# Expert capacities in multiples of 8 and 16, and row gathers rounded up to 16 rows, in a mixture-of-experts block

## The chip, the cores and the metric

The kernel runs on one core of one Trainium2 chip. The metric is the device time of one execution in microseconds (us). A run's profile is one execution of the program, recorded by the hardware profiler; its span is the time from the first to the last instruction of that record.

## The reference

One layer on 2048 tokens of width 1024, in float32. A mixer (a short gated convolution and a gated DeltaNet) and its output projection are added to `x`; then comes a hierarchical mixture of experts with a residual, and a last RMSNorm. What the change touches is the mixture:

```
group  = argmax(h @ router_group_w)                  # 4 groups
top 2  = top_k(softmax(h @ router_expert_w in group), 2)   # 8 experts in a group, 32 in all
gate   = group_prob * top_p / sum(top_p)
out[t] = sum over its 2 experts of gate * ((silu(h[t] @ w_gate[e]) * (h[t] @ w_up[e])) @ w_down[e])
y      = rms_norm(x + out)
```

The 2048 tokens give 4096 pairs of token and expert. Each of the 32 experts has 6.29 MB of float32 weights (1024x512 twice, 512x1024 once), 201 MB in all, and each is read once.

## The kernel before

The mixer takes roughly the first 1150 us. The change acts on what follows.

**Places.** Experts are ranked by their number of tokens, and the list `CAPS` (line 725) says for each rank how many places ("columns") the program computes, whatever the data: the first three ranks have 128, rank 3 has 216, and it falls to 112 for rank 31. (The first three are experts picked early from half of the tokens; a list of overflow blocks at the end of the program takes what doesn't fit. In this execution that loop runs no block.) A rank with more than 128 places has two chunks, one of 128 rows and one of the rest. There are 51 chunks: 13 ranks have one, 19 have two. Places without a token carry a row number past the last token: gathers clip it to token 2047, scatters skip it.

**Order.** The ranks run as jobs in this order, big and small ones in turn, so that ranks 29, 30 and 31 come last:

```
0 1 2 28 3 27 4 26 5 25 6 24 7 23 8 22 9 21 10 20 11 19 12 18 13 17 14 16 15 29 30 31
```

**One job**, in the order of its data:

- `load_part` (line 757): SP loads the expert's weights in 20 steps through ten staging buffers `mst` of 512 KB; ACT and DVE split each into two f16 halves (`split`, line 91; profile lines 92 and 93), `wgu` and `wd`. A load is issued when its buffer is free. Jobs ahead of the current one are loaded while it computes.
- `gather` (line 1046): POOL issues one indirect DMA for each chunk that fetches the token rows (4 KB each, both f16 halves) from `h2_d` into `xr` (line 1050), one row to a partition, and one for each chunk that fetches the gates `gs` (line 1055).
- `turn` (line 1059): TensorE transposes the rows into `xT` (line 1066), DVE copies them out.
- `gate_up` (line 1071): 192 matmuls with weights as the stationary operand and `n` columns of `xT` moving (line 1081), `n` being the rank's places. ACT and DVE make `ac` from the result.
- `down` (line 1107): a rank with one chunk takes `ac` as the stationary operand and moves 512 columns of `wd` (24 matmuls, line 1116); `n` is then no number of moving columns. A rank with two chunks has 96 matmuls with `n` moving columns (line 1151) and transposes back (line 1138). ACT scales the result by the gate into `yo` (lines 1125, 1142).
- `add` (line 1091): POOL issues one indirect DMA for each chunk that adds `yo` to the rows of `acc_d` in memory (line 1094).

ACT, DVE and POOL work each in their own program order.

**The end.** When rank 30 has been scattered, its tokens, those of rank 29 and of rank 31 are gathered from `acc_d` again, one gather for each rank with as many rows as it has places (`rows_of`, line 1420; rank 31's tile is `mst`, those of 29 and 30 are called `end`). Behind these on POOL's queue stand eight gathers of 128 rows for other tokens (`load_late`, line 1391, tile `xw`), and SP stores half of the first eight tiles at that time. ACT squares the tiles in the order `end` of 29, `end` of 30, four of `xw`, rank 31's, four of `xw`; DVE normalises; the stores follow. The last three stores are indirect DMAs on POOL, for ranks 29, 30 and 31 (`store_rows`, line 1431), and each waits until the one before it has landed.

Of the kernel before, what the change touches and what calls it, by code (L numbers as in the profile page):

```python
# [38 lines left out]
def hybrid_block(ctx, tc, x, mix_g, w_in, ca_w, ca_g, dn_w, a_log, dt_bias, dn_g, w_out,  # L39
# [675 lines left out]
    if dbg.get("stop") == "y":  # L715
# [6 lines left out]
    NST = 2  # L722
    C1 = P

    CAPS = [C1, C1, C1, 216, 188, 176, 172, 164, 160, 156, 152, 148, 148, 144, 144, 144, 140, 136, 136, 136,
            132, 132, 128, 128, 124, 124, 124, 120, 120, 120, 116, 112]
    NB2 = 2 * NE
    LAST = 3
    ACS = 4.0
# [63 lines left out]
    V.memset(on16, 1.0)  # L793
    iot = rt.tile([P, max(CAPS)], F32, name="iot")
    G.iota(iot, pattern=[[1, max(CAPS)]], base=0, channel_multiplier=0, allow_small_or_imprecise_dtypes=True)
    mhalf = rt.tile([P, 4], F32, name="mhalf")
# [3 lines left out]
    caps = rt.tile([NE, NE], F32, name="caps")  # L800
    for r, c in enumerate(CAPS):
        if r == 0 or CAPS[r - 1] != c:
            G.memset(caps[:, r:], float(c))
# [8 lines left out]

    CM = max(CAPS)
    tabT = psB.tile([NE, CM], F32, name="tabT", tag="b")
    tabE = rt.tile([NE, CM], F16, name="tabE")
    tabG = rt.tile([P, NE, 2], I32, name="tabG")
    tabS = rt.tile([P, NE, 2], I32, name="tabS")
    gix = rt.tile([P, NE, 2], I32, name="gix")
# [221 lines left out]
    class Job:  # L1040
        def __init__(self, key, chunks):
            self.key, self.chunks = key, chunks
            self.n = sum(c[3] for c in chunks)
            self.base = None

    def gather(J, pool, tag, end=S):
        J.xr, J.gs = [], []
        for ix, gx, sx, cw in J.chunks:
            xr = pool.tile([P, 2, KT, P], F16, name="xr", tag=tag)
            G.indirect_dma_start(out=xr[0:cw].rearrange("p a k c -> p (a k c)"), out_offset=None, in_=h2_d[0:end, :],  # L1050
                                      in_offset=IO(ap=ix, axis=0))
            J.xr.append(xr)
        for ix, gx, sx, cw in J.chunks:
            g = o2.tile([P, 1], F32, name="gs", bufs=6)
            G.indirect_dma_start(out=g[0:cw], out_offset=None, in_=gt_d[0:end * NE, :], in_offset=IO(ap=gx, axis=0))  # L1055
            J.gs.append(g)
        yield 1
# [280 lines left out]
    for r in order:  # L1338
        ch = []
        for i, cw in enumerate((min(CAPS[r], P), CAPS[r] - P)):  # L1340
            if cw > 0:
                ch.append((tabG[0:cw, r, i:i + 1], gix[0:cw, r, i:i + 1], tabS[0:cw, r, i:i + 1], cw))
        jobs.append(Job(r, ch))

    def fetch(J):
        yield from gather(J, o1, "hh")
# [239 lines left out]
```

## Time and profile before

| what | value |
|---|---|
| three timed runs | 1956.95, 1954.14, 1949.02 us (median 1954.14) |
| the profiled execution | 1948.9 us, its span 1947.1 us |
| mean granted TensorE clock | 0.962 of full speed |
| memory traffic | 330.27 MB, mean 170 GB/s |
| busy share of the span: TensorE matmuls, DVE, ACT, POOL | 90%, 72%, 52%, 22% |

The jobs take the time from some 1165 us to the end of the span. "Granted clock" is the share of TensorE's full speed that the throttle allowed. "DMA share" is the mean busy share of the core's 16 DMA engines; the time of overlapping packets can take it above 1. "Landing" is the time from an indirect DMA's issue to its data being there; the profile has it for about half of them.

### The profile page before, as it was taken

The page shows a single profiled execution, that of the slowest core. Times are in us where ns is not written, and L with a number is a line of the kernel's source. Part 1 is how long each engine was busy: PE and PEld are TensorE (multiplying, and loading weights), DVE is VectorE, ACT ScalarE, POOL GpSimd, SP SyncE. Part 2 cuts the span into 40 slices and gives each one's busy share as a digit, 9 for nine tenths or more (in the row PEclk, how much of TensorE's full clock was granted, in tenths as well). Part 3 has the DMA queues.
Part 4 walks back from the last instruction along what each step waited for, and adds up shares of the span by engine and source line. Part 5 has one row for each costly group of instructions (what it writes and reads, how often), then busy time and mean ns, then how long its engine had stood idle before and what let it go on. Part 6 is the DMA issues. An engine that isn't in the chain of part 4 may idle for free.

```text
span 1947.1 us, 41829 instructions
## 1 busy us (share of the span) xinstructions
PE 1752.6 (90%) x16221; PEld 1199.0 (62%) x16221; DVE 1403.5 (72%) x2713; ACT 1007.2 (52%) x1676; POOL 426.7 (22%) x375
## 2 busy tenths in 40 slices
PE   6789999999999999999999969999899999999840
PEld 5455555555555554444454438888788899999730
DVE  8889888888888745322344768777778888888732
ACT  5655434444444424211233637766667767777621
POOL 1321111121111100000000013223322344344343
PEclk9889999999999999999999979999999999999975
DMA  4122001001001105002255967999999999999873
GB/s 143 67 69 53 11 15 46 16 13 46 20 11 37 36 19 165 28 12 60 98 175 189 346 233 258 334 308 306 303 320 359 354 335 340 351 341 317 285 225 142
DMA packets 203597, 330.27 MB, mean 170 GB/s; under 512 B 44590, under 2 KB 98935, under 8 KB 203394
## 3 DMA queue, kind: packets, MB, share of 16 engines
q1 hardware_dynamic: 178738, 271.20, 40.9%
q0 software_dynamic: 20128, 47.30, 9.5%
q10 hardware_dynamic: 4528, 9.06, 1.2%
q8 instruction: 129, 2.11, 0.4%
q14 instruction: 74, 0.61, 0.1%
HBM read 276.05 MB, written 54.82 MB: 170 GB/s over the span
## 4 chain that ended last, share of the span: by engine, by line
PE 29%; DMA 20%; DVE 8%; issue 5%; ACT 5%; POOL 1%; SPq 1%; ACTq 0%; DVEq 0%; POOLq 0%
PE acc L134 11%; DMA mst<-in_w_up_dram 10%; PE a L1081 8%; DMA mst<-in_w_down_dram 5%; PE a L988 5%; DMA mst<-in_w_gate_dram 3%; DVE wgu L93 3%; ACT wgu L92 2%; DVE wd L93 1%; PE pn L548 1%; DMA end<-acc_d,tabG 1%; ACT yo L1142 1%; DMA mst<-acc_d,bix 1%; PE pl L1138 1%; SPq L766 1%
## 5 line engine op out<-in xcount | busy, mean ns | idle before, releaser
L134 PE MATMUL acc<-hT,whl 128*128 128x512 f16 x2640 | 635.3, 381 | 0.2 <-DVE hT L203 0.2
L134 PEld LDWEIGHTS <-whl 128*128 128x128 f16 x2640 | 252.9, 99 | 248.4 <-issue 11.4
L1081 PE MATMUL a<-xT,wgu 128*128 128x128 f16 (+17 forms) x6144 | 394.7, 227 | 3.3 <-DVE sl L1088 2.4
L1081 PEld LDWEIGHTS <-wgu 128*128 128x128 f16 x6144 | 389.3, 99 | 9.5 <-issue 3.5
L93 DVE SCALAR_TENSOR_TENSOR wgu<-mst,gw,wgu 128x1024 f16<-128x1024 f32 x256 | 317.5, 1276 | 19.9 <-ACT wgu L92 17.6
L92 ACT ACTIVATE wgu<-mst,gw 128x1024 f16<-128x1024 f32 x256 | 280.8, 1139 | 36.0 <-DMA mst<-in_w_up_dram 33.7
L988 PE MATMUL a<-wo,yb 128*128 128x512 f16 x768 | 176.3, 381 | 0.0
L93 DVE SCALAR_TENSOR_TENSOR wd<-mst,wd 128x1024 f16<-128x1024 f32 x128 | 154.2, 1215 | 3.6 <-ACT wd L92 3.5
L1094 POOL DMA_INDIRECT acc_d<-yo,tabS x50 | 95.9, 1918 | 265.9 <-ACT yo L1142 191.8
L92 ACT ACTIVATE wd<-mst 128x1024 f16<-128x1024 f32 x128 | 131.3, 1047 | 24.3 <-DMA mst<-in_w_down_dram 24.1
L1151 PE MATMUL a<-ac,wd 128*128 128x144 f16 (+12 forms) x1824 | 136.9, 230 | 4.9 <-ACT ac L92 3.9
L1151 PEld LDWEIGHTS <-wd 128*128 128x128 f16 x1824 | 124.4, 98 | 8.3 <-issue 6.5
L988 PEld LDWEIGHTS <-yb 128*128 128x128 f16 x768 | 72.2, 98 | 79.6 <-issue 3.0
L294 DVE SCALAR_TENSOR_TENSOR cv<-raw,pcol,cv 128x512 f32<-128x512 f32 x144 | 117.1, 815 | 1.6
L1050 POOL DMA_INDIRECT xr<-h_d,tabG x51 | 61.5, 1206 | 179.2 <-PE t L1066 159.0
L1088 DVE SCALAR_TENSOR_TENSOR sl<-a,sl 128x128 f32<-128x128 f32 (+17 forms) x128 | 38.3, 300 | 78.1 <-ACT sl L1087 77.6
L1087 ACT ACTIVATE sl<-a 128x128 f32<-128x128 f32 (+17 forms) x128 | 35.7, 280 | 108.9 <-PE a L1081 108.9
L1116 PE MATMUL pl<-wd,ac 128*128 128x512 f16 (+4 forms) x312 | 78.6, 397 | 6.1 <-ACT ac L92 4.8
L382 DVE TENSOR_TENSOR pr<-Ts,fs 32x1 f32<-32x1 f32 (+14 forms) x240 | 76.6, 319 | 4.4 <-DMA fs<-dscr 0.7
L1055 POOL DMA_INDIRECT gs<-gt_d,gix x51 | 74.3, 1457 | 15.7 <-issue 15.4
L545 ACT ACTIVATE osq<-acv 128x512 f32<-128x512 f32 x16 | 10.1, 628 | 125.3 <-DVE acv L543 125.3
L1138 PE MATMUL pl<-id,yt 128*128 128x128 f32 (+13 forms) x304 | 52.8, 292 | 23.4 <-ACT yo L1142 17.2
(357 smaller groups left out, 2536.6 us busy)
## 6 DMA issues: line engine op xcount, KB each, us to landing
mst<-in_w_gate_dram SPq DMA_DIRECT2D x256, 256.0 KB
mst<-in_w_up_dram SPq DMA_DIRECT2D x256, 256.0 KB
mst<-in_w_down_dram SPq DMA_DIRECT2D x128, 512.0 KB
wst<-in_w_in_dram SPq DMA_DIRECT2D x28, 512.0 KB
xt<-in_x_dram SPq DMA_DIRECT2D x16, 512.0 KB
ydr<-yh SPq DMA_DIRECT2D x64, 128.0 KB
x<-in_x_dram SPq DMA_DIRECT2D x16, 512.0 KB
yb<-ydr SPq DMA_DIRECT2D x16, 512.0 KB
```

The lines of the kernel that those rows point to most:

```text
L92: A.activation(hi, src, AF.Copy, scale=scale)
L93: (eng or V).scalar_tensor_tensor(lo, src, scale, hi, op0=OP.mult, op1=OP.subtract)
L134: T.matmul(acc, w[:, i, k, :], hT[b][:, j, k, :], start=(n == 0), stop=(n == 3 * KT - 1))
L294: V.scalar_tensor_tensor(y, tap(j), pcol[:, q:q + 1], y, op0=OP.mult, op1=OP.add)
L382: V.tensor_tensor(q, Ts[:, 0:i, 0:i].rearrange("p j m -> p m j"), bc(fs[:, None, 0:i, i], [32, i, i]), op=OP.mult)
L988: T.matmul(po, yb[:, i, k, c * P:(c + 1) * P], wo[:, j, k, n * FF:(n + 1) * FF], start=(q == 0), stop=(q == 3 * KT - 1))
L1055: G.indirect_dma_start(out=g[0:cw], out_offset=None, in_=gt_d[0:end * NE, :], in_offset=IO(ap=gx, axis=0))
L1081: T.matmul(pg[:, q, 0:n], wq[:, i, k, q, f * P:(f + 1) * P], xT[:, j, k, 0:n], start=(z == 0), stop=(z == 3 * KT - 1))
L1094: st = G.indirect_dma_start(out=acc_d, out_offset=IO(ap=sx, axis=0), in_=yo[0:cw], in_offset=None, bounds_check=S - 1, oob_is_err=False, c ...
L1116: T.matmul(py[0:n], ac[:, i, k, 0:n], wd[:, j, k, q * FF:(q + 1) * FF], start=(z == 0), stop=(z == 3 * FF // P - 1))
L1138: T.transpose(py[0:cw, c * P:(c + 1) * P], yts[d2][:, u, off:off + cw], id32)
L1151: T.matmul(pg[:, u, 0:n], wd[:, i, k, d * P:(d + 1) * P], ac[:, j, k, 0:n], start=(z == 0), stop=(z == 3 * FF // P - 1))
```

## The change

The sizes in `CAPS` become multiples of 8: 92 places more in all (4524 to 4616). Ranks 24 to 30, which had 124 to 116, have 128. Rank 31 keeps 112. Ranks 3, 27, 28 and 29 gain 8, rank 30 gains 12; ranks 4, 6, 7, 9, 11, 12, 16, 20, 21 and 24 to 26 gain 4. Gathers of rows and of gates take the chunk's rows rounded up to 16; transposes, matmuls and scatters take the chunk's own number. Nothing is reordered.

```diff
-    CAPS = [C1, C1, C1, 216, 188, 176, 172, 164, 160, 156, 152, 148, 148, 144, 144, 144, 140, 136, 136, 136,
-            132, 132, 128, 128, 124, 124, 124, 120, 120, 120, 116, 112]
+    CAPS = [C1, C1, C1, 224, 192, 176, 176, 168, 160, 160, 152, 152, 152, 144, 144, 144, 144, 136, 136, 136,
+            136, 136, 128, 128, 128, 128, 128, 128, 128, 128, 128, 112]
...
+    def even(n):
+
+        return -(-n // 16) * 16
+
     def gather(J, pool, tag, end=S):
         J.xr, J.gs = [], []
         for ix, gx, sx, cw in J.chunks:
+            cw = even(cw)
             xr = pool.tile([P, 2, KT, P], F16, name="xr", tag=tag)
...
         for ix, gx, sx, cw in J.chunks:
+            cw = even(cw)
             g = o2.tile([P, 1], F32, name="gs", bufs=6)
...
-                ch.append((tabG[0:cw, r, i:i + 1], gix[0:cw, r, i:i + 1], tabS[0:cw, r, i:i + 1], cw))
+                ch.append((tabG[0:even(cw), r, i:i + 1], gix[0:even(cw), r, i:i + 1], tabS[0:cw, r, i:i + 1], cw))
```

## Rows read from the trace of the kernel before

**Rows 1.** page, busy time (us, share of the span) and instructions of each engine
```profile
PE 1752.6 (90%) x16221; PEld 1199.0 (62%) x16221; DVE 1403.5 (72%) x2713; ACT 1007.2 (52%) x1676; POOL 426.7 (22%) x375
```

**Rows 2.** busy time by stretch: us, each engine, PEclk, DMA share, GB/s
```profile
1200.00:1250.00 50.00, 46.05 (x564) 38.09 (x563) 41.94 (x52) 36.78 (x51) 11.17 (x8) 0.97 1.04 349
1250.00:1300.00 50.00, 48.57 (x602) 45.21 (x600) 40.83 (x54) 36.24 (x52) 17.16 (x11) 1.00 1.03 319
1300.00:1350.00 50.00, 45.45 (x578) 41.82 (x576) 39.61 (x53) 33.48 (x48) 14.91 (x9) 0.97 0.99 316
1350.00:1400.00 50.00, 44.79 (x599) 41.20 (x598) 35.81 (x48) 32.05 (x45) 14.58 (x9) 1.00 0.99 302
1400.00:1450.00 50.00, 44.60 (x576) 40.22 (x574) 41.63 (x57) 35.51 (x53) 14.80 (x9) 0.97 0.98 332
1450.00:1500.00 50.00, 46.18 (x610) 41.73 (x609) 37.34 (x51) 32.68 (x48) 11.56 (x9) 0.93 0.94 319
1500.00:1550.00 50.00, 49.15 (x700) 44.90 (x698) 44.88 (x64) 40.48 (x58) 15.87 (x11) 1.00 1.02 353
```

**Rows 3.** timeline of POOL, scatters of five experts: start, us, [idle before]
```profile
1323.71 1.88 POOL L1094 DMA_INDIRECT acc_d<-yo,tabS  x1 [15.85 <-ACT yo L1142]
...
1372.96 2.08 POOL L1094 DMA_INDIRECT acc_d<-yo,tabS  x1 [15.85 <-ACT yo L1142]
...
1422.25 1.89 POOL L1094 DMA_INDIRECT acc_d<-yo,tabS  x1 [16.63 <-ACT yo L1142]
...
1512.54 3.15 POOL L1094 DMA_INDIRECT acc_d<-yo,tabS  x1 [10.72 <-ACT yo L1142]
...
1552.81 2.19 POOL L1094 DMA_INDIRECT acc_d<-yo,tabS  x1 [7.65 <-ACT yo L1142]
```

**Rows 4.** chain that ended last, 1190 to 1460: start, us, what
```profile
1207.93 8.73 DMA mst<-in_w_up_dram
...
1385.14 14.03 DMA mst<-in_w_down_dram
...
1446.24 14.32 DMA mst<-in_w_up_dram
```

**Rows 5.** line 1094, landing of scatters: all; rank 24's alone; rank 29's alone
```profile
DMA to landing us min/median/max: 7.6/9.6/19.0
...
DMA to landing us min/median/max: 19.0/19.0/19.0
...
DMA to landing us min/median/max: 7.6/7.6/7.6
```

**Rows 6.** line 1432, the three last stores: ranks 29, 30, 31
```profile
DMA to landing us min/median/max: 4.4/4.4/4.4
...
DMA to landing us min/median/max: 9.5/9.5/9.5
...
DMA to landing us min/median/max: 3.7/3.7/3.7
```

**Rows 7.** busy time by stretch while those stores run, columns as in 2
```profile
1920.00:1925.00 5.00, 0.00 (x0) 0.00 (x0) 0.00 (x0) 0.00 (x0) 2.59 (x3) 0.50 0.83 302
...
1930.00:1935.00 5.00, 0.00 (x0) 0.00 (x0) 0.00 (x0) 0.00 (x0) 0.00 (x0) 0.50 0.20 59
```

**Rows 8.** timeline of PE: matmuls of ranks 27 and 4
```profile
1274.83 8.41 PE L1081 MATMUL a<-xT,wgu 128*128 128x120 f16 x157
...
1290.14 15.68 PE L1081 MATMUL a<-xT,wgu 128*128 128x188 f16 x192
...
1313.39 2.10 PE L1151 MATMUL a<-ac,wd 128*128 128x188 f16 x24
```

**Rows 9.** timeline of POOL: rank 30's scatter and the gather behind it
```profile
1865.40 2.17 POOL L1094 DMA_INDIRECT acc_d<-yo,tabS  x1 [8.81 <-ACT sl L1087]
...
1879.32 1.02 POOL L1421 DMA_INDIRECT mst<-acc_d,tabG  x1 [10.67 <-DMA acc_d<-yo,tabS]
```

**Rows 10.** tile end, gathers of ranks 29 and 30 at the end
```profile
DMA to landing us min/median/max: 8.6/12.0/15.4
```

## The prediction

> **What bounds the kernel now.** I read the page's busy times first: TensorE is busy for 90% of the span [rows 1], so added columns may cost time. A mean hides the stages, so I then cut the job stage into stretches of 50 us [rows 2]. From 1500 us on TensorE works for 49.15 of 50 us while 353 GB/s come in: there it is the bound. From 1250 to 1500 us it sits idle for 1.4, 4.6, 5.2, 5.4 and 3.8 us of each 50 (the stretch less the first number), and the memory moves only 302 to 332 GB/s. That stage waits for something that isn't full bandwidth.
>
> Third, the starts of scatters on POOL give the pace of the jobs [rows 3]: between the first scatters of ranks 4, 5 and 6 lie 49.3 us each (a big rank and one of 124 places), between those of ranks 8 and 9 (with 22, which has 128) 40.3. Ranks 5 and 6 have 20 and 16 places more than rank 9; at 288 matmuls of 0.41 ns a place (worked out in part 2) that is at most 2.4 us, not 9. Fourth, the chain of waits says what is late: loads of weights. A link of it takes 8.7 us early on, but 14.0 and 14.3 us beside the transfers of ranks 24 and 25, which have 124 rows [rows 4].
>
> Fifth, the landing of the scatters: 9.6 us in the median, 19.0 for rank 24's 124 rows [rows 5]. The cleanest case is the end, where three stores run one after the other with nothing else to do: 120 rows land in 4.4 us, 116 rows in 9.5, 112 rows in 3.7 [rows 6]. While the 116 rows move, the 16 DMA engines are busy for 0.20 of the time, which is some three engines' worth, and carry 59 GB/s; in the stretch before, 0.83 and 302 GB/s [rows 7]. So 116 and 124 rows, multiples of 4 alone, go to few engines; 112, 120 and 128 to nearly all.
>
> The Trainium skill (DMA: Bandwidth & Descriptors, section "Why a DMA increments its semaphore by 16 and not by 1") states the rule: a transfer goes to the largest number of engines up to 16 that divides the slowest dimension of both its sides, here the rows. By it 116 and 124 get 4 engines, 120 gets 15, 112 and 128 get 16; the trace agrees, 9.5 us against 4.4 and 3.7. The section also names an exception, some direct copies issued from GpSimd that spread any count over 16 engines; if it held for these indirect ones it would leave the change nothing but its columns, which is the second rival below.
>
> **Part 1, the middle: ranks 26, 25 and 24 go from 124 rows to 128.** Removed are three gathers and three scatters on few engines, all within the stage from 1250 to 1500 us. Weight loads are cut over all engines, so a load ends with its slowest engine, and the staging buffers come free late. Second chunks are rounded in the gathers too, but those of the middle (60, 48, 44, 36 rows) have few rows on any engine, and I cost that at nothing; it is hidden under the job computed meanwhile, and a gather that landed later than a job lasts would cost its excess.
>
> - By rate: from 1250 to 1500 us the mean is (319+316+302+332+319)/5 = 317.6 GB/s, 79.4 MB; some 40 more gathered rows are 0.2 MB. At 349 GB/s, which the stretch from 1200 reached with no transfer of 124 rows, that takes 228 us: 22 us less.
> - By TensorE, the upper end: idle time of the five stretches 20.4 us; granted clock 0.97, 0.97 and 0.93 costs another 1.5 + 1.5 + 3.5 us. Of these 26.9 us the columns that this stage gains (below) take 3.0: 23.9 us less.
> - Low end: the stretch from 1200 us also waited, 3.95 us and 1.5 of clock. If that much stays in each of the four stretches from 1300 us, whose own sum is 19.0 + 6.5 = 25.5 us, 3.7 us are won.
>
> The early stretch holds experts of 128 places, with less matmul time for each byte of weights than the pairs after it, so its wait is too much for them. I take 16, nearer to the rate.
>
> The Trainium skill (same page, section "Where 436 GB/s comes from") gives a ceiling for the rate, some 358 GB/s as one core's share of the memory. At 358 the 79.6 MB take 222 us, past TensorE's bound, so the sum by it would have 23.9 in place of 16; the trace shows 353 [rows 2] and doesn't contradict it.
>
> **Part 2, columns.** 192 matmuls of 188 columns take 15.68 us, 157 of 120 columns 8.41: 81.7 and 53.6 ns, 0.41 ns a column, and still falling below 128; 24 of the second matmul at 188 take 2.10 us, 87 ns each, close to the same [rows 8]. So 4 places cost 192 x 4 x 0.41 = 0.32 us, and 0.16 more where the down step moves them too (96 matmuls, two chunks): 0.48. In the stage that TensorE bounds: ranks 9, 21, 20, 11, 12 and 16, 6 x 0.48 = 2.9; rank 29 (8 places) 0.6; rank 30 (12) 0.9: 4.4 us. Rank 30's may hide, since its scatter waited 8.8 us on ACT [rows 9]. I take 4.0 (3.5 to 4.5). The columns before 1500 us (ranks 27, 4, 26, 25, 6, 24, 7: 3.0 us; 28 and 3: 1.6) are free as long as weights set the pace; without that they cost 4.6. For a rank with one chunk the down step's 24 matmuls move 512 columns as before: nothing. The larger tables, 8 columns more, are a few DVE and matmul instructions, under 1 us, during routing: nothing.
>
> **Part 3, the end: rank 30 goes from 116 rows to 128, rank 29 from 120.** Three transfers stand one behind the other.
>
> - Rank 30's scatter starts at 1865.40 us and the gather that waits for it at 1879.32 [rows 9]: 13.9 us. Rank 29's took 7.6, the median is 9.6 [rows 5]: 4.3 to 6.3 us less, taken 5.3. All that stands behind that gather on POOL moves up, and TensorE and ACT aren't in the way, as the last rank's scaling waits for the same gather.
> - Rank 30's gather lands after 15.4 us, rank 29's, issued just before it, after 8.6 [rows 10]. Up to 5.5 us less; but eight gathers of 512 KB and the stores of SP share the engines, and ACT squares what they bring next. By volume nearly nothing might be won: 1 to 5.5, taken 3.5.
> - Rank 30's store needs 9.5 us; at 3.7 to 4.4 [rows 6] 5.1 to 5.8 less, taken 5.3. Rank 29's goes from 15 or so engines to 16: 0.2.
>
> Sum 14.3 (10.4 to 17.8).
>
> **Sum.** 16 + 14.3 - 4.0 = 26.3 us less. Against the profiled execution that is 1948.9 - 26.3 = 1922.6 us; against the median of the runs, which lies 5.2 above it, 1927.8. I forecast 1925. The forecast's own range: 1948.9 - 23.9 - 17.8 + 3.5 = 1911 at best, 1954.1 - 3.7 - 10.4 + 4.5 = 1944.5 at worst.
>
> **Rivals.**
>
> - *The middle is bound by volume anyway.* The mean DMA share there, 0.94 to 1.03, is little below the 1.02 of the good stretch [rows 2], which speaks against idle engines; then only the end gains: 14.3 - 4.0 = 10.3, 1939 to 1944 us. Against it: 317.6 against 353 GB/s, and the 14 us links.
> - *Slower: rows aren't what spreads a transfer, columns are all that is left.* The long landings would come from the place in the queue (rank 30's gather stood behind two others). Its place is TensorE from 1500 us on, 98% busy; its price 4.4 us there, and 9.0 where the early columns show as well: 1953 to 1963 us. It decides if the shorter transfers give back less than those 4.4 to 9.0 us. Against it stands the lone store of 116 rows, which had no queue ahead of it.
> - *Padding that collides.* Rows gathered beyond the tokens all fetch token 2047. Were each gather late by a job's length, transposes would wait; but a gather has a whole job, some 20 us, to land. I count it with the slower rival.
>
> **Chances.** Forecast 0.68, volume 0.20, slower 0.12. 0.5%, about what a measurement of this kernel can tell from no change, is 9.8 us: faster than that is nearly all of the forecast and some 0.12 of the volume rival, together 0.79; within it the rest of that rival and half of the slower one, 0.16; slower 0.05. The range takes in the forecast's own and the volume rival: 1910 to 1946.
>
> **What would show it.** Right: scatters of ranks 24 to 26 land near 10 us, not 19; stretches from 1300 to 1500 us carry some 345 GB/s with TensorE idle under 3 us; 43 to 45 us from rank 4 to rank 5; rank 30's store in some 4 us; 0.33 us more for each 4 columns of a `gate_up` after 1500 us. Wrong: landings are short but the rate stays at 317 GB/s (volume), or 128 rows at the end still need 9 us (spread). The end's sum fails if the `xw` gathers set the pace there.

## The result and the profile after

The changed kernel takes 1925.26 us (median of four runs, 1924.55 to 1927.41), the kernel before 1951.58 (median of four, 1946.77 to 1956.95): a ratio of 0.9866, with a 95% interval of 0.9836 to 0.9896. The forecast was 1925. The profiled execution took 1924.55 us, its span is 1922.7.

TensorE is as busy as before [rows 1], in a shorter span (page, busy time of each engine):

```profile
PE 1754.9 (91%) x16221; PEld 1198.1 (62%) x16221; DVE 1403.2 (73%) x2713; ACT 1004.8 (52%) x1676; POOL 432.0 (22%) x367
```

Busy time by stretch, columns as in [rows 2]:

```profile
1250.00:1300.00 50.00, 49.04 (x573) 45.00 (x572) 38.88 (x51) 34.63 (x49) 15.19 (x9) 1.00 1.01 339
1300.00:1350.00 50.00, 48.76 (x624) 44.84 (x622) 41.45 (x55) 36.27 (x52) 17.73 (x11) 1.00 0.99 331
1350.00:1400.00 50.00, 48.62 (x646) 44.49 (x644) 42.83 (x59) 35.89 (x54) 16.13 (x10) 1.00 1.03 335
1400.00:1450.00 50.00, 48.58 (x658) 44.45 (x656) 39.84 (x57) 34.04 (x52) 15.30 (x10) 1.00 1.02 343
1450.00:1500.00 50.00, 47.96 (x660) 43.64 (x658) 43.82 (x61) 39.02 (x56) 16.32 (x10) 1.00 1.02 344
```

In [rows 2] TensorE idled for 3.8 to 5.4 us in each stretch from 1300 to 1500 us; now for 1.2 to 2.0, the granted clock is 1.00 throughout, and 331 to 344 GB/s come in for 302 to 332 (the prediction's marks were some 345 and under 3 us idle). How late weights reach TensorE is seen in the waits, in total, times and longest. From 1250 to 1500 us, in the kernel before, ACT stands ahead of its splitting until weights have landed, 30.9 us in these two rows, and TensorE waits for the tile `pl` until ACT, which works in program order, has read it into `yo`:

```profile
ACT wd L92 <- DMA mst<-in_w_down_dram: 16.1, 10, 3.0
ACT wgu L92 <- DMA mst<-in_w_up_dram: 14.8, 16, 2.8
...
PE pl L1138 <- ACT yo L1142: 12.9, 5, 3.5
```

In the changed kernel TensorE's matmuls no longer have that wait, and of ACT's 0.9 us are left:

```profile
ACT wgu L92 <- DMA mst<-in_w_up_dram: 0.5, 1, 0.5
ACT wd L92 <- DMA mst<-in_w_down_dram: 0.4, 2, 0.2
```

The same on POOL's timeline, first scatters of ranks 4, 5, 6, 8 and 9, as in [rows 3]:

```profile
1329.01 4.32 POOL L1100 DMA_INDIRECT acc_d<-yo,tabS  x1 [11.10 <-ACT yo L1148]
...
1373.43 4.42 POOL L1100 DMA_INDIRECT acc_d<-yo,tabS  x1 [10.82 <-ACT yo L1148]
...
1417.77 4.42 POOL L1100 DMA_INDIRECT acc_d<-yo,tabS  x1 [10.82 <-ACT yo L1148]
...
1504.34 3.15 POOL L1100 DMA_INDIRECT acc_d<-yo,tabS  x1 [10.78 <-ACT yo L1148]
...
1547.91 3.23 POOL L1100 DMA_INDIRECT acc_d<-yo,tabS  x1 [9.73 <-ACT yo L1148]
```

The pairs take 44.4 and 44.3 us where they took 49.3. On the chain that ended last, the longest load between 1190 and 1460 us is now 10.6 us, where [rows 4] have 14.0 and 14.3:

```profile
1333.32 10.61 DMA mst<-in_w_down_dram
```

The end, POOL's timeline: rank 30's scatter, the gather behind it, and the last three stores (ranks 29, 30, 31):

```profile
1856.01 1.65 POOL L1100 DMA_INDIRECT acc_d<-yo,tabS  x1 [9.27 <-ACT yo L1131]
1862.38 0.98 POOL L1427 DMA_INDIRECT mst<-acc_d,tabG  x1 [4.72 <-DMA acc_d<-yo,tabS]
...
1903.53 0.97 POOL L1438 DMA_INDIRECT out_dram<-end,tabS  x1 [0.30 <-issue]
1907.34 0.97 POOL L1438 DMA_INDIRECT out_dram<-end,tabS  x1 [2.83 <-DMA out_dram<-end,tabS]
1910.82 0.95 POOL L1438 DMA_INDIRECT out_dram<-mst,tabS  x1 [2.51 <-DMA out_dram<-end,tabS]
```

From scatter to gather 6.4 us (13.9 in [rows 9]). Rank 30's store starts at 1907.34 and the next at 1910.82: 3.5 us, against the 9.5 of [rows 6].

**Where the time went.** The jobs can be cut at POOL's starts, from the first row gather to the end of the span. "To 8" means up to the first scatter of rank 8, and so on; g is the gather behind rank 30's scatter, s the first of the last three stores. One profile of each kernel, two of the changed one; the experiments below explain the other names. In us:

| kernel | first job | to 8 | to 14 | to 15 | to 29 | to 30 | to g | to s | to end |
|---|---|---|---|---|---|---|---|---|---|
| before | 27.6 | 326.2 | 259.2 | 47.8 | 29.1 | 16.8 | 13.9 | 42.8 | 24.9 |
| after | 33.4 | 310.6 | 262.9 | 44.1 | 27.4 | 17.2 | 6.4 | 41.2 | 19.2 |
| after, 2nd profile | 32.8 | 312.8 | 262.7 | 44.1 | 27.4 | 15.9 | 6.5 | 40.7 | 19.1 |
| mid_only | 33.1 | 309.3 | 259.8 | 48.9 | 28.6 | 15.8 | 14.0 | 45.1 | 26.2 |
| end_only | 33.7 | 320.1 | 259.8 | 43.9 | 26.8 | 17.3 | 6.5 | 39.6 | 18.3 |
| mid_end | 32.8 | 307.0 | 259.7 | 43.9 | 26.8 | 17.3 | 6.4 | 39.8 | 20.1 |
| no_round | 33.5 | 310.6 | 262.9 | 44.1 | 27.4 | 15.9 | 6.3 | 39.8 | 19.2 |
| round_only | 34.3 | 321.6 | 259.9 | 43.9 | 26.7 | 16.3 | 13.9 | 42.7 | 27.5 |
| r117 | 32.5 | 323.4 | 259.7 | 46.5 | 26.7 | 15.4 | 6.8 | 38.4 | 18.9 |
| r118 | 32.9 | 321.7 | 259.8 | 51.5 | 28.2 | 15.6 | 23.5 | 48.7 | 29.1 |
| sc_only | 26.7 | 326.2 | 259.3 | 49.0 | 27.9 | 15.7 | 14.9 | 44.9 | 27.4 |
| spread_free | 27.9 | 337.4 | 259.3 | 43.9 | 32.6 | 15.1 | 6.2 | 38.5 | 19.1 |
| rows_only | 33.9 | 340.0 | 259.8 | 43.7 | 32.8 | 15.4 | 6.4 | 37.9 | 20.6 |
| cols_more | 26.7 | 309.9 | 266.8 | 44.1 | 27.4 | 17.2 | 6.3 | 40.3 | 19.2 |

Between the first two rows: +5.7 in the first job, -15.6 to rank 8, +3.7 to 14, -3.7 to 15, -1.6 to 29, +0.4 to 30, -15.0 at the end, in all 26.1 us less. The forecast's sum was 26.3, made up otherwise. Two entries stand nowhere in it: the first job (last section), and the 3.7 us won in the stretch from 14 to 15. Single profiles vary: the last three columns add up to 81.6 us in the kernel before and to 85.3 in mid_only, whose end is the same.

### The profile page after: what moved, and what is told of

Its sections match the earlier page's. It is cut to its first block, busy times and chain, and to the rows that moved or that the text cites. A ratio compares the mean times of both kernels' runs of the same rounds, so it can differ in the third digit from the quotient of the medians.

```text
span 1922.7 us, 41830 instructions
## 1 busy us (share of the span) xinstructions
PE 1754.9 (91%) x16221; PEld 1198.1 (62%) x16221; DVE 1403.2 (73%) x2713; ACT 1004.8 (52%) x1676; POOL 432.0 (22%) x367
## 4 chain that ended last, share of the span: by engine, by line
PE 38%; DMA 14%; DVE 11%; ACT 5%; issue 5%; SPq 1%; POOL 1%; another core or an unknown queue 1%; ACTq 0%; DVEq 0%; POOLq 0%
PE acc L134 13%; PE a L1087 11%; PE a L988 5%; DMA mst<-in_w_up_dram 5%; DMA mst<-in_w_down_dram 5%; DVE wgu L93 3%; DMA mst<-in_w_gate_dram 2%; ACT wgu L92 2%; PE pl L1122 1%; PE pn L548 1%; PE t L1072 1%; DVE pr L382 1%; DMA wst<-in_w_out_dram 1%; DVE xT L1073 1%; SPq L766 1%
## 5 line engine op out<-in xcount | busy, mean ns | idle before, releaser
L134 PEld LDWEIGHTS <-whl 128*128 128x128 f16 x2640 | 253.2, 99 | 250.3 <-issue 14.3
L1087 PE MATMUL a<-xT,wgu 128*128 128x128 f16 (+9 forms) x6144 | 399.5, 227 | 6.0 <-issue 3.4
L1087 PEld LDWEIGHTS <-wgu 128*128 128x128 f16 x6144 | 393.7, 99 | 12.5 <-issue 7.1
L92 ACT ACTIVATE wgu<-mst,gw 128x1024 f16<-128x1024 f32 x256 | 277.0, 1137 | 14.5 <-DMA mst<-in_w_up_dram 14.3
L1100 POOL DMA_INDIRECT acc_d<-yo,tabS x50 | 110.2, 2205 | 239.7 <-ACT yo L1148 169.6
L1157 PE MATMUL a<-ac,wd 128*128 128x136 f16 (+7 forms) x1824 | 138.2, 231 | 1.1 <-issue 0.5
L1094 DVE SCALAR_TENSOR_TENSOR sl<-a,sl 128x128 f32<-128x128 f32 (+9 forms) x128 | 38.8, 304 | 94.1 <-ACT sl L1093 86.8
L1093 ACT ACTIVATE sl<-a 128x128 f32<-128x128 f32 (+9 forms) x128 | 36.3, 285 | 135.0 <-PE a L1087 111.0
L1122 PE MATMUL pl<-wd,ac 128*128 128x512 f16 (+1 forms) x312 | 75.8, 389 | 8.6 <-ACT ac L92 6.7
L92 ACT ACTIVATE ac<-sl 128x128 f16<-128x128 f32 (+9 forms) x128 | 40.6, 318 | 64.3 <-DVE sl L1094 62.7
L1061 POOL DMA_INDIRECT gs<-gt_d,gix x51 | 69.1, 1355 | 15.6 <-issue 15.3
```

The source lines that it names most:

```text
L92: A.activation(hi, src, AF.Copy, scale=scale)
L134: T.matmul(acc, w[:, i, k, :], hT[b][:, j, k, :], start=(n == 0), stop=(n == 3 * KT - 1))
L1087: T.matmul(pg[:, q, 0:n], wq[:, i, k, q, f * P:(f + 1) * P], xT[:, j, k, 0:n], start=(z == 0), stop=(z == 3 * KT - 1))
L1100: st = G.indirect_dma_start(out=acc_d, out_offset=IO(ap=sx, axis=0), in_=yo[0:cw], in_offset=None, bounds_check=S - 1, oob_is_err=False, c ...
L1122: T.matmul(py[0:n], ac[:, i, k, 0:n], wd[:, j, k, q * FF:(q + 1) * FF], start=(z == 0), stop=(z == 3 * FF // P - 1))
L1157: T.matmul(pg[:, u, 0:n], wd[:, i, k, d * P:(d + 1) * P], ac[:, j, k, 0:n], start=(z == 0), stop=(z == 3 * FF // P - 1))
```

## The experiments

The theory: an indirect transfer whose row count has only small divisors up to 16 goes to few engines; while it runs, weight loads lag, and what waits for it waits long. Rival A: the middle is bound by volume. Rival B: rows aren't what spreads a transfer, columns are all that is left. Rival C: the rounding of the gathers does the work. Medians are given against the kernel before in the same set of runs.

### The middle alone and the end alone

mid_only is the kernel before with three sizes changed:

```diff
-            132, 132, 128, 128, 124, 124, 124, 120, 120, 120, 116, 112]
+            132, 132, 128, 128, 128, 128, 128, 120, 120, 120, 116, 112]
```

> The kernel before with ranks 24, 25 and 26 alone at 128 places in place of 124. If the middle was held by transfers of 124 rows on few DMA engines, nearly the whole gain of that stage comes with these three: some 16 us less than before (1935 where before gives 1951), the scatters of these ranks land near 10 us, and from the first scatter of rank 3 to that of rank 7 it takes 178 us as in the changed kernel, where it was 195. If volume or something else in the change (rounded gathers, wider tables) made the gain, this run stays within 3 us of before.

1938.84 against 1952.08 us: 0.9942 (0.9921 to 0.9962), 13.2 us less. Busy time by stretch:

```profile
1300.00:1350.00 50.00, 48.60 (x631) 44.69 (x629) 41.69 (x55) 36.59 (x53) 18.21 (x11) 1.00 1.01 335
1350.00:1400.00 50.00, 48.58 (x649) 44.46 (x647) 42.19 (x58) 34.41 (x53) 15.32 (x9) 1.00 1.01 341
1400.00:1450.00 50.00, 48.23 (x661) 43.96 (x659) 40.86 (x57) 36.00 (x53) 15.99 (x10) 1.00 1.01 345
```

Twelve places more, and the stretches that carried 316, 302 and 332 GB/s [rows 2] carry 335 to 345: rival A falls.

end_only changes one size:

```diff
-            132, 132, 128, 128, 124, 124, 124, 120, 120, 120, 116, 112]
+            132, 132, 128, 128, 124, 124, 124, 120, 120, 120, 128, 112]
```

> The kernel before with rank 30 alone at 128 places in place of 116. If three transfers of 116 rows in a row set the end, this run is 13 to 15 us faster than before: about 5 less in the scatter, 3 to 5 in the gather, 5 to 6 in the store, less 1 us for 12 more columns; the middle keeps its 195 us from rank 3 to rank 7. If the row count isn't what makes those transfers long, the store still needs 9 us and the time is before's plus 1.

1927.02 against 1952.08: 0.9885 (0.9853 to 0.9917), 25.1 us less, well above what was expected. The table shows why: besides the end, the stretch from 14 to 15 fell from 47.8 to 43.9 us and the next from 29.1 to 26.8, long before rank 30 is scattered. There its *first* gather runs, the one that fetches its rows for its own job (it is the 50th of 51 row gathers and is issued at 1784.60 us in the kernel before, 1784.90 here). Busy time from 1790 to 1820 us, first the kernel before:

```profile
1790.00:1800.00 10.00, 9.79 (x148) 9.28 (x146) 9.11 (x12) 7.57 (x12) 4.54 (x3) 1.00 1.05 262
1800.00:1810.00 10.00, 9.62 (x150) 9.26 (x148) 7.93 (x15) 6.22 (x10) 0.95 (x1) 1.00 0.93 262
1810.00:1820.00 10.00, 6.22 (x64) 5.35 (x62) 7.10 (x8) 7.55 (x10) 0.43 (x1) 0.76 1.03 373
```

and end_only:

```profile
1790.00:1800.00 10.00, 9.78 (x148) 9.27 (x146) 10.00 (x14) 8.21 (x14) 5.31 (x3) 1.00 1.04 355
1800.00:1810.00 10.00, 9.62 (x151) 9.26 (x149) 7.02 (x13) 6.40 (x10) 1.20 (x2) 1.00 1.03 348
1810.00:1820.00 10.00, 9.85 (x165) 9.30 (x163) 9.83 (x12) 9.59 (x14) 3.74 (x2) 1.00 1.03 361
```

Behind the gather of 116 rows the memory moves 262 GB/s for 20 us; TensorE then has nothing to do for 3.8 of 10 us, at a granted clock of 0.76. With 128 rows neither shows. It is the picture of the middle once more, in a stage that the prediction, from its 98% of busy TensorE at 1500 us, had put down as TensorE's.

### Does the divisor count, or the size? 117 and 118 rows

Two neighbours of 116: 117 is 9 x 13, 118 is 2 x 59. Their largest divisors up to 16 are 13 and 2; that of 116 is 4. If only the size counted, both would be as slow as 116.

```diff
-            132, 132, 128, 128, 124, 124, 124, 120, 120, 120, 116, 112]
+            132, 132, 128, 128, 124, 124, 124, 120, 120, 120, 117, 112]    # r117; 118 in r118
```

> The kernel before with rank 30 at 117 places, one more than before. 117 is 9 x 13, no multiple of 2. If a transfer is spread over the largest number of engines up to 16 that divides its rows, 117 rows take 13 engines with 9 rows each: the last-but-one store lands in about 4.5 us in place of 9.5, rank 30's scatter in some 7 and its first gather no longer holds the weights (44 us from rank 14 to rank 15, not 48); in all 20 to 25 us less than before. If it is multiples of 8 or 16 that are fast, 117 is as slow as 116 or slower: 1951 or more. The Trainium skill (DMA: Bandwidth & Descriptors, section Why a DMA increments its semaphore by 16 and not by 1) states the first rule.

> The kernel before with rank 30 at 118 places, two more than before. 118 is 2 x 59. By the divisor theory its rows go to 2 engines with 59 rows each, against 4 with 29 for the 116: the store doubles from 9.5 to some 19 us, the scatter from 13 to some 26, the gather at the end from 15 to 25 or 30, and the time is 20 to 40 us above before. If places count by multiples of 4 or 8, or if the spread is even, 118 is like 116: 1951 and a store of 9 to 10 us.

r117: 1927.22 against 1954.99, 0.987 (0.9829 to 0.991). r118: 1973.78 against 1954.99, 1.01 (1.0071 to 1.013). One place apart, 46.6 us. POOL's timeline of r117, the stores of ranks 30 and 31:

```profile
1913.76 0.99 POOL L1432 DMA_INDIRECT out_dram<-end,tabS  x1 [3.69 <-DMA out_dram<-end,tabS]
1917.89 0.96 POOL L1432 DMA_INDIRECT out_dram<-mst,tabS  x1 [3.15 <-DMA out_dram<-end,tabS]
```

and of r118:

```profile
1944.31 1.65 POOL L1432 DMA_INDIRECT out_dram<-end,tabS  x1 [3.73 <-DMA out_dram<-end,tabS]
1958.00 0.95 POOL L1432 DMA_INDIRECT out_dram<-mst,tabS  x1 [12.04 <-DMA out_dram<-end,tabS]
```

From store to store 4.1 us with 117 rows, 13.7 with 118. While the latter runs (busy time of r118):

```profile
1951.00:1956.00 5.00, 0.00 (x0) 0.00 (x0) 0.00 (x0) 0.00 (x0) 0.00 (x0) 0.50 0.11 44
```

Read as engines at work, a DMA share of 0.11 is 1.8 of 16, where 116 rows had 0.20 [rows 7], 3.2 engines. So the divisor decides how long a store takes, and rival B falls. Two sizes were off. 118 rows take 1.4 times as long as 116, not twice, and cost 18.8 us in all, less than the 20 to 40 expected. And r117's stretch from 14 to 15 is 46.5 us, where 44 was expected. Busy time of r117, whose first gather of rank 30 starts at 1787.96:

```profile
1790.00:1800.00 10.00, 9.79 (x145) 9.19 (x142) 9.73 (x11) 8.47 (x11) 2.57 (x2) 1.00 1.03 223
...
1810.00:1820.00 10.00, 7.09 (x97) 6.31 (x95) 9.15 (x12) 7.55 (x9) 0.00 (x0) 1.00 1.01 344
```

Beside 117 rows the memory still falls to 223 GB/s for 10 us, and TensorE idles for 2.9 of 10. With 13 engines for 16 the divisor alone doesn't say why; that stays open.

### The rounding: alone, and left out

no_round is the changed kernel with

```diff
     def even(n):
-        return -(-n // 16) * 16
+        return n
```

> The changed kernel without the rounding of gathers to 16 rows (the new places alone). If the rounding is worth nothing, as the prediction costs it, this run lies within 2 us of the changed kernel, 26 us under before. If second chunks on few engines hold the loads too, it gives back some of the middle's 16 us, 3 us or more.

1921.32 against 1952.08: 0.986 (0.9823 to 0.9897), as the changed kernel's 0.9866. round_only is the reverse, the old sizes with `even` in the gathers (tables 224 wide, and the gathers of the end with the rank's own number of rows; the definition of `even` and these two are left out here):

```diff
...
+            cw = even(cw)
...
-                ch.append((tabG[0:cw, r, i:i + 1], gix[0:cw, r, i:i + 1], tabS[0:cw, r, i:i + 1], cw))
+                ch.append((tabG[0:even(cw), r, i:i + 1], gix[0:even(cw), r, i:i + 1], tabS[0:cw, r, i:i + 1], cw))
```

> The kernel before with the rounding of gathers alone: gathers of all ranks take multiples of 16 rows (those of 124, 120 and 116 rows take 128), scatters, the gathers and stores at the end and all columns stay as before. The tables are 224 wide as in the changed kernel. If both the gather and the scatter of ranks 24 to 26 hold the loads, this run gains a part of the middle's 16 us, 4 to 8, as the scatter with its read and write moves more. If the scatters alone hold them, it gains under 2. In both cases the end keeps its 82 us from rank 30's scatter on.

1947.63 against 1952.08: 0.9977 (0.9958 to 0.9996). Gathers of 128 rows for 124 win nothing in the middle (321.6 us to rank 8, with 320.1 to 323.4 in end_only, r117 and r118, whose middle is unchanged too). But the stretch from 14 to 15 falls to 43.9 us, as in end_only: there the gather alone was at fault, as its scatter comes later. Rival C falls for the change as a whole, since its sizes leave the rounding nothing large to mend.

### Rows and columns apart

Three kernels keep the columns (matmuls) of the kernel before and give the transfers 128 rows; the added rows are skipped by their index. As the scatter reads all 128 partitions of `yo`, the last 32 are zeroed first. sc_only does it for the scatters of ranks 24 to 26 alone, zeroed by DVE (here and below the lines that take the transfers' row counts from these lists are left out):

```diff
+                if q == 0 and J.chunks[0][2].shape[0] > n:
+                    V.memset(J.yo[0][96:P], 0.0)
...
-                ch.append((tabG[0:cw, r, i:i + 1], gix[0:cw, r, i:i + 1], tabS[0:cw, r, i:i + 1], cw))
+                ch.append((tabG[0:cw, r, i:i + 1], gix[0:cw, r, i:i + 1], tabS[0:(P if cw == 124 else cw), r, i:i + 1], cw))
```

> The kernel before with the scatters of ranks 24, 25 and 26 alone spread over 128 rows: gathers stay at 124 rows and matmuls at 124 columns, the four rows more are set to zero by DVE and carry a row number that scatters skip. If the scatters alone hold the weights in the middle (the rounded gathers alone won nothing there), this run gains all that mid_only gains, 13 us, and rank 8's scatter comes 341 us after the first gather, not 354. If gather and scatter each hold them and either is enough, it gains under 4.

spread_free does it for every transfer of ranks 24 to 30:

```diff
+                rw = P if 112 < cw < P else cw
-                ch.append((tabG[0:cw, r, i:i + 1], gix[0:cw, r, i:i + 1], tabS[0:cw, r, i:i + 1], cw))
+                ch.append((tabG[0:rw, r, i:i + 1], gix[0:rw, r, i:i + 1], tabS[0:rw, r, i:i + 1], cw))
```

> The kernel before with all its columns as they were, but every transfer of ranks 24 to 30 (gathers of rows and gates, scatters, gathers and stores at the end) over 128 rows; rows without a place are zero or clipped, and scatters skip them. If columns cost on TensorE and rows on the DMA engines alone, it has the whole gain of mid_end and saves its 24 columns, 1 to 2 us: 1913 to 1916 where before gives 1952 to 1955. If rows moved in vain cost as much as columns do, it is no better than the changed kernel, 1922 to 1925.

rows_only zeroes with ACT instead, and leaves the gathers of ranks 24 to 26 at 124:

```diff
+                    A.activation(J.yo[0][96:P], bc(iot[96:P, 0:1], [P - 96, D]), AF.Copy, scale=0.0)
...
+                rw = P if 112 < cw < P else cw
+                rg = cw if cw == 124 else rw
```

> All columns as before. Ranks 24, 25 and 26: scatters over 128 rows, gathers at 124 rows. Ranks 27 to 30: every transfer over 128 rows. Rows without a place are zero and skipped; ACT zeroes them just ahead of its own first write to that tile, so that no engine waits that didn't wait before (in sc_only and spread_free DVE did, 5 to 6 us a time). If scatters alone hold the weights in the middle, rank 8's scatter comes some 341 us after the first gather; if the gathers of 124 rows hold them as well, or columns of 128 are what matters, it stays at 350 to 355. The end shall be that of mid_end, 93 us from rank 29's scatter minus nothing for columns: 15 to 16 from rank 29 to 30, then 64 to 66. In all 1913 to 1916 where before gives 1952 in the first case, 1926 to 1930 in the second.

sc_only 1952.57 against 1944.86: 1.0037 (1.0021 to 1.0052). spread_free 1937.02 against 1944.86: 0.995 (0.9935 to 0.9966). rows_only 1950.95 against 1952.5: 0.9983 (0.9971 to 0.9996). All three miss what was expected of them: none wins anything in the middle, and the added zeroing is a wait of its own. Waits of sc_only's DVE, 1300 to 1480 us (in total, times, longest):

```profile
DVE yo L1122 <- DMA acc_d<-yo,tabS: 18.0, 3, 7.1
```

and of rows_only's ACT:

```profile
ACT yo L1122 <- DMA acc_d<-yo,tabS: 29.3, 3, 10.4
```

The zeroing can't write `yo` before the last scatter out of that buffer has landed, and everything behind it on its engine, the splitting of weights too, waits along. TensorE's largest wait of sc_only from 1250 to 1500 us is for DVE's copies of the transposed rows:

```profile
PE t L1066 <- DVE xT L1067: 12.5, 3, 5.9
```

The 12.9 us that it waited for `pl` before are 3.1 here: the old wait went, and one of its size came. The scatters themselves did get short, 8.9 to 11.5 us in sc_only for ranks 24 to 26, near the 10 us that the prediction named as a mark (the changed kernel's trace lists no landings); rank 24's took 19.0 before [rows 5]. ACT's waits for weights fell too, from 30.9 us to 10.5 in sc_only and 0.4 in spread_free, at unchanged columns. But rows_only, which has the same transfers in the middle as sc_only, has 2.2: an engine that stands still for the zeroing gives the loads time. So these runs don't tell whether rows alone suffice in the middle, with the columns as they were; that stays open. At the end they are clear: with rank 30 computing 116 columns and moving 128 rows, 6.2 and 6.4 us to g and 19.1 and 20.6 us from s to the end, as with 128 columns. There rows make the gain, the columns only come along.

### What the late columns cost

cols_more is the changed kernel with 8 places more for ranks 17 to 21, 40 in all:

```diff
-    CAPS = [C1, C1, C1, 224, 192, 176, 176, 168, 160, 160, 152, 152, 152, 144, 144, 144, 144, 136, 136, 136,
-            136, 136, 128, 128, 128, 128, 128, 128, 128, 128, 128, 112]
+    CAPS = [C1, C1, C1, 224, 192, 176, 176, 168, 160, 160, 152, 152, 152, 144, 144, 144, 144, 144, 144, 144,
+            144, 144, 128, 128, 128, 128, 128, 128, 128, 128, 128, 112]
```

> The changed kernel with ranks 17 to 21 at 144 places in place of 136: 8 columns more in five jobs of the stage that TensorE bounds, and the same 16 rows in their second gathers. At 0.41 ns a column and 288 matmuls that is 0.94 us a rank: 4.7 us from rank 8's scatter to rank 15's, so 311 to 312 where the changed kernel has 307. If columns are hidden behind the weights there too, the stretch stays at 307.

1918.54 against 1944.86: 0.9857 (0.9827 to 0.9888), which can't be told from the changed kernel's ratio. The profile can tell: from rank 8 to 15 it takes 311.0 us, the changed kernel 307.0, so 3.9 us for 40 places. TensorE's timeline, 186 matmuls of `gate_up` in cols_more:

```profile
1628.17 11.79 PE L1087 MATMUL a<-xT,wgu 128*128 128x144 f16 x186
```

and in the changed kernel:

```profile
1634.27 11.17 PE L1087 MATMUL a<-xT,wgu 128*128 128x136 f16 x186
```

0.62 us for 8 columns, 0.42 ns for each column of a matmul; the prediction had 0.41 from [rows 8].

### Only what gains

mid_end puts mid_only and end_only together: the kernel before with four sizes of 128, and none of the other places.

```diff
-            132, 132, 128, 128, 124, 124, 124, 120, 120, 120, 116, 112]
+            132, 132, 128, 128, 128, 128, 128, 120, 120, 120, 128, 112]
```

> The kernel before with ranks 24, 25, 26 and 30 at 128 places, all other places as before and no rounding: the two runs mid_only and end_only in one. If their gains add (13 and 25 us by the medians) the time is 1914, some 11 us under the changed kernel, and the difference is what the other 64 places of the change cost. If the two gains overlap, so that the changed kernel's 1925 is what is to be had, this run is within 4 us of 1925.

The changed kernel ran beside it once more, as after_again:

> The changed kernel once more, on the chip and against the runs of before that mid_end has: 1925 again, ratio 0.987. It is the yardstick for mid_end, and its profile is a second look at the first job, whose matmuls lost some 5 us in the changed kernel's profile and not in the profile of before.

mid_end takes 1915.59 against 1954.99 us: 0.9814 (0.9783 to 0.9844). after_again takes 1921.82: 0.9841 (0.9807 to 0.9875). The intervals against before overlap, but every run of mid_end (1912.18 to 1917.70) lies below every run of after_again (1918.98 to 1926.00). It beats both kernels, and its 39.4 us are about those of mid_only and end_only added (13.2 + 25.1 = 38.3). Its stores of ranks 30 and 31:

```profile
1894.92 1.00 POOL L1432 DMA_INDIRECT out_dram<-end,tabS  x1 [3.62 <-DMA out_dram<-end,tabS]
1898.42 0.95 POOL L1432 DMA_INDIRECT out_dram<-mst,tabS  x1 [2.51 <-DMA out_dram<-end,tabS]
```

## Why the prediction was right

**What bounds.** The mechanism was read rightly from the landings. It is shown by rows alone at the end and for rank 30's first gather; in the middle rows and columns changed together (mid_only), and there it rests on the rate, on the waits for weights and on the landings. The links of [rows 4] were a choice: the same chain has one of 14.0 us at 1288.35, behind rank 26's gather of 124 rows, which agrees, but also one of 11.5 at 1225.06, ahead of any 124 rows, where the prediction gave 8.7 for the early ones:

```profile
1225.06 11.49 DMA mst<-in_w_up_dram
...
1288.35 14.04 DMA mst<-in_w_down_dram
```

The Trainium skill (DMA: Bandwidth & Descriptors, section "Why a DMA increments its semaphore by 16 and not by 1") gives the largest divisor up to 16 as the number of engines; r117 and r118 agree (stores of 4.1 and 13.7 us). Its exception, some direct copies that spread any count over 16 engines, doesn't show in these indirect transfers: the stores of 116 and 118 rows take 9.5 and 13.7 us where that of 117 takes 4.1. The 358 GB/s that the prediction cites as a ceiling isn't one here: the row from 1810 to 1820 us of the kernel before has 373.

**Part 1, the middle: 16 us, measured 13.7.** From the first gather to rank 8's scatter take 354.8 us as a mean of before, end_only, r117, r118 and round_only, and 341.1 of mid_only and mid_end. mid_only's timed gain of 13.2 us agrees. By these runs the term is 2.3 us too large; its bounds (3.7 to 23.9) held. But all of these profiles except the first have the loss of the last section, which weighs on the two kinds of kernel differently. Without it on either side, the kernel before takes 353.8 us and cols_more, up to rank 8 the changed kernel, 336.6: 17.2 less, early columns included. So it isn't settled in which direction the term missed. That the rounding is worth nothing held too.

**Part 2, columns.** Late ones: 4.0 us, measured 3.1 (to 14), 0.3 (to 15) and 0.7 (to 29), the changed kernel against mid_end and end_only: 4.1. Rank 30's columns, 0.9 of the prediction's 4.4, aren't in that, since mid_end and end_only have them too. From 29 to 30 the six profiles with 128 columns take 16.8 us as a mean (15.9 to 17.3), the other eight 15.8 (15.1 to 16.8): about that, within the scatter. The early columns "are free as long as weights set the pace" was said for the wrong kernel: after the change weights no longer set it. The mean to rank 8 is 344.5 us in the changed kernel (its two profiles and no_round), 341.1 in mid_only and mid_end, all five with the loss in the first job: 3.4 us of the 4.6 are paid.

**Part 3, the end: 14.3 us, measured 18.4.** Means of the four profiles with rank 30 at 116 rows throughout (before, mid_only, round_only, sc_only) against the three of the changed sizes (after, after_again, no_round): 14.2 to 6.4 us up to g (7.8; predicted 5.3, since the best case was taken from rank 29's landing of 7.6 us [rows 5], and 6.4 is less than that), 43.9 to 40.6 up to s (3.3; predicted 3.5, with an upper end of 5.5 for which [rows 10] would have given 15.4 - 8.6 = 6.8), 26.5 to 19.2 for the stores (7.3; predicted 5.5 with rank 29's). Between the two profiles first shown it is 15.0.

**What the sum lacked.** Rank 30's first gather: 4.7 us in the stretch from 14 to 15 (48.6 as a mean of before, mid_only and sc_only, 43.9 in end_only) and 1.7 in the next (28.5, 26.8), 6.4 in all. Part 3 took rank 30 only from its scatter on, though [rows 3] and [rows 4] had shown what such a gather does to the loads beside it.

Together -13.7 + 3.4 + 4.1 - 18.4 - 6.4 = -31.0 us; the two timings gave -26.3 and -33.2. That the forecast of 26.3 less meets the first timing is luck in part: errors of both signs stood against each other, a missed gain of 6.4 and an end 4.1 too small, a middle 2.3 too large and 3.4 of early columns. They leave 4.7 us, less than the 6.9 by which the two timings of the same kernel differ.

**The rivals.** Volume: refuted by mid_only. Slower, columns alone left: refuted by r117 and r118, and by rows_only at the end. Padding that collides: no_round and the changed kernel don't differ, and mid_end, whose added places are all padding, is the fastest of all.

## What to carry to other kernels

Before the size of an indirect transfer is trimmed to the data, look at the divisors of its row count: 117 rows stored in 4.1 us here, 118 in 13.7, and behind one gather of 116 rows the memory moved 262 GB/s for 20 us, where 128 rows left 348 to 355. Follow every transfer of the job with that count, its first gather too, not only the one that stands at the end. Then change only the counts that are bad: four of 32 sizes gave 39 us, and the changed kernel with its other places ran 6 us longer.

## What the runs showed besides

**A loss in the first job.** The 192 `gate_up` matmuls of the first job run through in some profiles and falter in others, with the same instructions. TensorE's timeline in the changed kernel:

```profile
1168.77 4.52 PE L1087 MATMUL a<-xT,wgu 128*128 128x128 f16 x53
1174.43 0.22 PE L1087 MATMUL a<-xT,wgu 128*128 128x128 f16 x1 [1.14 <-issue]
1175.16 0.22 PE L1087 MATMUL a<-xT,wgu 128*128 128x128 f16 x1 [0.51 <-issue]
1175.88 0.22 PE L1087 MATMUL a<-xT,wgu 128*128 128x128 f16 x1 [0.51 <-issue]
1177.31 9.21 PE L1087 MATMUL a<-xT,wgu 128*128 128x128 f16 x133 [1.21 <-issue]
```

and in the kernel before:

```profile
1166.90 12.23 PE L1081 MATMUL a<-xT,wgu 128*128 128x128 f16 x189
```

The first job takes 26.7 to 27.9 us in four of the fourteen profiles and 32.5 to 34.3 in the others. It doesn't go with the edit: sc_only, spread_free and cols_more, which ran one after the other on one chip, are all without it, the nine other experiments all have it, and of the two profiles first shown before is without it and after has it. "issue" means that the engine waited for nothing that the profile shows, so the cause stays open. To the kernel before it hardly mattered: up to rank 8 it took 353.8 us without the loss, and the four with the loss and the same middle (end_only, r117, r118, round_only) 353.7 to 355.9. In the changed kernel it shows: 344.0 to 345.6 us with it (its two profiles and no_round), 336.6 without (cols_more, on another chip). That the weights had hidden it, and no longer do, is a reading of these times and no experiment.

**Few engines carry more each.** 116 rows moved 59 GB/s at a DMA share of 0.20, by estimate 18 GB/s for each of 3.2 engines; 118 rows 44 GB/s at 0.11, 25 GB/s for each of 1.8. That goes with 118 rows not taking twice as long as 116; why an engine carries more is open.
